# Attention heads emitted in steps, and the row of 1/rms spread behind the first transposes

## The chip, the cores and the metric

The kernel runs on one core of a Trainium2 chip. The metric is device time in microseconds (us) of one execution; lower is better. The engines have short names: PE (TensorE, matmuls and transposes), DVE (VectorE), ACT (ScalarE), POOL (GpSimd) and SP (SyncE, which issues the DMAs). Each engine works through its own list of instructions in order, and waits at an instruction until what it needs has been signalled by the others.

## The reference, cut to what matters

The program computes two layers of a decoder trunk in float32 on x of 512 tokens by 1024 features. Each layer is half an FFN, a mixer, half an FFN. The change lies in the mixer:

```python
h = rms_norm(x, mix_norm[l])
(nq, nkc, nvc, nks, nvs, nkw, nvw, ngate, sq, sk, sv, wq, wk, wv, bgate) = jnp.split(
    h @ w_in[l], SPLIT_POINTS, axis=-1)
y_nsa = nsa_attention(...)                       # 8 heads: compressed, selected, window
y_sb = stick_breaking_attention(sq, sk, sv)      # 4 heads, no softmax
y_swa = swa_sink_attention(wq, wk, wv, ...)      # 4 heads, window 128, sinks
g = sigmoid(bgate).reshape(B, S, 3, D)
merged = g[:, :, 0] * (y_nsa @ w_up_nsa[l]) + g[:, :, 1] * (y_sb @ w_up_sb[l]) + g[:, :, 2] * (y_swa @ w_up_swa[l])
x = x + merged @ w_out[l]
```

A stick-breaking head weighs key s for query t by beta_ts times the product of (1 - beta_tj) over s < j < t, with beta the sigmoid of the score; the product is a scan along a row. rms_norm divides each token by its root mean square; the kernel multiplies by 1/rms after the matmuls.

## The kernel before, in words

Matmuls are split into two parts: a float32 value a is hi + lo, with hi rounded to the matmul's short type by ACT (whi, ghi) and lo = a - hi by DVE (wlo, glo), and a product takes three matmuls (hi hi, lo hi, hi lo; lines 204 to 206 and 623 to 625). PE results go to eight PSUM banks of 128 partitions by 512 floats. `psum(...)` says which banks serve which kind of tile in turn: acc for accumulators, f for transposes and small products, s for scores, t for transposed weights, o for head outputs, c for the compress product. A tile waits until the last reader of the earlier tile in its bank is done.

`mix_front` emits the first part of the mixer of a layer: six projections `project(l, 0)` to `project(l, 5)` of h, each with four accumulators (one for each block of 128 tokens) over four loads of weights; after each, its accumulators are emptied (`evacuate`, DVE line 644, times 1/rms by a column, rcol), heads are normed and transposed, and heads of attention are emitted. `more(n)` adds early gates between them: `gate_early` makes one accumulator of gate logits (lines 204 to 206, from ghi and glo), multiplies it on DVE by the row of 1/rms (line 1045, tile gs), takes the sigmoid on ACT (line 1029) and stores it by SP into DRAM (gkept, line 1030). gs has one buffer. The first `more` makes two gates, in the first two acc banks, 4 and 5.

`nrm.means()` sums the squares by four small matmuls (line 242), works out rcol on DVE, and makes a diagonal of it (line 249, four instructions). `nrm.spread()` multiplies ones by that diagonal on PE (line 254), which gives 1/rms as a row in all partitions; ACT copies it out (line 256, tile rrow).

`transposed` (lines 682 to 693) makes hi and lo of the rows (ACT line 682, POOL line 683, tile st), transposes them on PE (line 691, tile f) and copies the result by ACT (line 693). sq has 16 such transposes, sk 32.

`stick_breaking` gives one head at a time: four scores (PE lines 716 and 717, tile s), two sigmoids of each (ACT lines 785 and 786), the diagonal block masked (POOL line 788, DVE line 789), the scan (DVE line 791), the product (POOL line 792, tile e); then the weights are transposed (PE lines 739 to 748, tile t), split (ACT line 727, DVE line 728, tile pt) and multiplied by v (PE line 733, tile o).

The whole is traced under `tile.TileContext(nc, schedule_with_timeline_sim=True)`: a scheduler decides the order on each engine from the emitted program, with the order of emission as a guide and its own costs. So the order of the code is not the order of the engines, and instructions are often drawn far ahead of where they are written.

Of the kernel before, what the change touches and what calls it, by code (L numbers as in the profile page):

```python
# [9 lines left out]
F32 = mybir.dt.float32  # L10
# [8 lines left out]
P = 128  # L19
# [75 lines left out]
def trunk(ctx, tc, I, out):  # L95
# [679 lines left out]
    def stick_breaking(q, k, v):  # L775

        for h in range(SBH):
# [3 lines left out]
            for t in range(NT):  # L781
# [11 lines left out]
                probs.append(beta)  # L793
            o = bank("o")
# [4 lines left out]
    def sliding(q, k, v, sinks):  # L799

        for h in range(SWH):
            if h % 2 == 0:
                y = unit("y")
            g = h // 2
            tab = unit("tt")[:, 0:SWW]
            rows = I["bias_rows"]
            sp.dma_start(tab, bass.AP(rows.tensor, rows.offset + (NH + h) * (RW + SRW) + RW, [[1, P], [1, SWW]]))
            neg = sm.tile([P, NT], F32, name=nm("neg"), tag="neg", bufs=3)
            den = sm.tile([P, NT], F32, name=nm("den"), tag="den", bufs=3)
            sk = sm.tile([P, NT], F32, name=nm("sk"), tag="sk", bufs=3)  # L810
            es = []
            for t in range(NT):
                p = bank("s")
                k0 = max(t - 1, 0) * P
                n = P if t == 0 else 256
                for i in range(2):
                    pe.matmul(p[:, 0:256], q[h][:, t * P : (t + 1) * P], k[g][i][:, k0 : k0 + 256], start=i == 0, stop=i == 1)
                e = unit(f"e{t}")[:, 0:n]
                dve.tensor_tensor_reduce(out=e, in0=p[:, 0:n], in1=tab[:, 0:n][:, ::-1], scale=-1.0, scalar=3e38, op0=ALU.add, op1=ALU.min, accum_out=neg[:, t : t + 1])
                es.append(e)  # L820

            dve.tensor_scalar(neg, neg, sinks[:, SWH + h : SWH + h + 1], None, ALU.min)
            dve.tensor_scalar(sk, neg, sinks[:, h : h + 1], None, ALU.add)
            for t in range(NT):
                exp(es[t], es[t], bias=neg[:, t : t + 1], scale=-1.0, accum_out=den[:, t : t + 1])
            exp(sk, sk)
            dve.tensor_tensor(den, den, sk, op=ALU.add)
            dve.reciprocal(den, den)
            for t in range(NT):
                pool.tensor_scalar(es[t], es[t], den[:, t : t + 1], 1.0, ALU.mult, ALU.mult)  # L830
            o = bank("o")
            pb = bank("t")
            pe.transpose(pb[:, 0:P], es[0], ident)
            pe.transpose(pb[:, P : 2 * P], es[1][:, 0:P], ident)
            pe.transpose(pb[:, 2 * P : 3 * P], es[1][:, P : 2 * P], ident)
            pe.transpose(pb[:, 3 * P : 4 * P], es[2][:, 0:P], ident)
            a = split_pt(pb, 0, 512)
            pb = bank("t")
            pe.transpose(pb[:, 0:P], es[3][:, P : 2 * P], ident)
            pe.transpose(pb[:, P : 2 * P], es[2][:, P : 2 * P], ident)  # L840
            pe.transpose(pb[:, 2 * P : 3 * P], es[3][:, 0:P], ident)
            b = split_pt(pb, P, 384)
            pv(o, v(g), 0, a, 0, 0, 256, True, False)

            for i, part in enumerate(b):
                pe.matmul(o[:, 256:512], v(g)[2], part[:, 256:512], start=False, stop=True, skip_group_check=True)
            for i, part in enumerate(a):
                pe.matmul(o[:, 128:384], v(g)[1], part[:, 256:512], start=False, stop=True, skip_group_check=True)
            for i, part in enumerate(b):
                pe.matmul(o[:, 256:512], v(g)[3], part[:, 0:256], start=False, stop=True, skip_group_check=True)  # L850
            finish_head(o, y, h)
            yield y
# [97 lines left out]
    def nsa(q, kk, v, vc, gates):  # L950
# [32 lines left out]
        ys = []  # L983
        for h in range(NH):
            if h % 2 == 0:
                y = unit("yn")
# [4 lines left out]
            o = bank("o")  # L991
# [18 lines left out]
            pool.tensor_tensor(e3, e3, den.unsqueeze(2).to_broadcast([P, NT, 32]), op=ALU.mult)  # L1010
            pb = bank("t")
# [6 lines left out]
            pe.matmul(o, vc[:, g].rearrange("p c d -> p (c d)"), part[0:64], start=True, stop=True, skip_group_check=True)  # L1018

            full_pv(o, scaled(chosen, h, 0), v(g), False, False)  # L1020
            full_pv(o, scaled(attend(h, kk[2 + g], tab), h, 1), v(2 + g), False, True)
            finish_head(o, y, h)
            if h % 2:
                ys.append(y)
# [42 lines left out]
    def mix_front(l, nrm, more):  # L1067
# [62 lines left out]
        for h, y in enumerate(sliding(wq, wk, wv, sinks)):  # L1130
            if h % 2:
                y_sw.append(y)
# [155 lines left out]
```

## Time and profile before

| | us |
|---|---|
| median of 3 runs | 2386.36 (2385.3 to 2389.08) |
| profiled execution, its own time | 2389.16 |
| its span | 2387.3 |
| PE busy | 2330.3 (98%) |
| DVE busy | 1749.4 (73%) |
| ACT busy | 1186.4 (50%) |
| POOL busy | 440.5 (18%) |
| mean granted clock of PE | 0.992 of full speed |

PE is busy in nearly the whole span, in every part of it; the other engines are full only in short stretches. In layer 0 the mixer's front begins near 393 us and its stick-breaking heads end near 545; in layer 1 the same comes some 1180 us later. The profiled execution is 2.8 us longer than the median.

### The profile page before, as it was taken

Reading aid. Unit: us, or ns where it says so; the run is one execution under the profiler, and the core shown is the slowest. Engines: PE = TensorE matmul, PEld = TensorE weight load, DVE = VectorE, ACT = ScalarE, POOL = GpSimd, SP = SyncE. Lnnn points to the kernel's source line nnn. Section 1 sums busy time; section 2 is a strip of 40 time slices with the busy share of each in tenths; the row PEclk is TensorE's granted clock in tenths of the full one; section 3 lists DMA queues with packets and bytes.
Section 4 is the critical chain, followed back from the end, with each engine's and each line's share of the span. In section 5 each row is a group of like instructions: output and inputs, shape, how many; then the busy total and the mean of one; then the engine's idle time right before and its main releaser. Section 6 shows DMA issues by size and latency. Waiting matters only on the chain.

```text
span 2387.3 us, 37809 instructions
## 1 busy us (share of the span) xinstructions
PE 2330.3 (98%) x14484; PEld 2066.2 (87%) x14484; DVE 1749.4 (73%) x3022; ACT 1186.4 (50%) x2145; POOL 440.5 (18%) x574
## 2 busy tenths in 40 slices
PE   8999999999999999999999999998999999999999
PEld 8988986887887799889899899778878878998997
DVE  8865864686777799658798568538867777994783
ACT  5533543454766555335455335335657664552451
POOL 1001001342333410010000100115234344001000
PEclk9999999999999999999999999999999999999999
DMA  4232333232323323323323332422423243233223
GB/s 160 96 106 82 103 118 112 76 124 91 98 94 119 115 80 107 104 83 107 109 86 105 111 96 87 144 79 86 143 70 104 77 140 102 74 112 109 96 90 96
DMA packets 83089, 244.15 MB, mean 102 GB/s; under 512 B 10197, under 2 KB 12034, under 8 KB 82908
## 3 DMA queue, kind: packets, MB, share of 16 engines
q1 hardware_dynamic: 82908, 241.73, 31.5%
q8 instruction: 114, 1.87, 0.3%
q14 instruction: 67, 0.55, 0.1%
HBM read 230.61 MB, written 11.08 MB: 101 GB/s over the span
## 4 chain that ended last, share of the span: by engine, by line
PE 88%; DVE 7%; issue 2%; ACT 1%; DMA 1%; POOL 1%; SPq 0%; DVEq 0%; ACTq 0%; POOLq 0%
PE X L392 20%; PE acc L206 13%; PE acc L204 13%; PE acc L205 12%; PE W L392 10%; PE Y L392 5%; PE acc L623 2%; PE acc L624 2%; PE acc L625 2%; PE o L733 2%; PE s L716 1%; PE s L717 1%; PE f L691 1%; DVE wlo L190 1%; PE c L891 1%
## 5 line engine op out<-in xcount | busy, mean ns | idle before, releaser
L189 ACT CAST whi<-wraw 128x1024 fp32r<-128x1024 f32 (+4 forms) x224 | 193.1, 866 | 397.3 <-PE acc L205 249.5
L190 DVE TENSOR_TENSOR wlo<-wraw,whi 128x1024 fp32r<-128x1024 f32 (+4 forms) x224 | 244.5, 1097 | 169.0 <-ACT whi L189 168.7
L392 ACT CAST whi<-u 128x1024 fp32r<-128x1024 f32 x156 | 163.8, 1050 | 283.0 <-DVE u L392 280.3
L204 PE MATMUL acc<-u,whi 128*128 128x512 f32 x704 | 276.9, 396 | 2.2 <-DVE gl L1150 2.2
L205 PE MATMUL acc<-u,whi 128*128 128x512 f32 x704 | 276.8, 394 | 0.0
L206 PE MATMUL acc<-u,wlo 128*128 128x512 f32 x704 | 276.6, 395 | 0.0
L392 DVE TENSOR_TENSOR wlo<-u,whi 128x1024 fp32r<-128x1024 f32 x164 | 204.5, 1247 | 14.8 <-ACT whi L392 14.3
L392 PE MATMUL X<-u,whi 128*128 128x256 f32 x1376 | 180.5, 284 | 3.7 <-ACT Y L392 3.0
L606 POOL TENSOR_TENSOR gl<-gl,e 128x512 f32<-128x512 f32 x32 | 55.9, 1747 | 690.7 <-DVE e L604 690.7
L392 PEld LDWEIGHTS X<-u,whi 128*128 128x128 f32 x1376 | 171.0, 189 | 7.0 <-ACT Y L392 3.4
L204 PE MATMUL acc<-u,ghi 128*128 128x512 f32 x384 | 162.3, 423 | 4.2 <-DVE gl L707 4.2
L206 PE MATMUL acc<-u,glo 128*128 128x512 f32 x384 | 159.5, 416 | 5.8 <-DVE glo L196 5.8
L204 PEld LDWEIGHTS acc<-u,whi 128*128 128x128 f32 x704 | 132.5, 188 | 34.3 <-DVE gl L1150 4.2
L206 PEld LDWEIGHTS acc<-u,wlo 128*128 128x128 f32 x704 | 132.4, 188 | 30.8
L205 PEld LDWEIGHTS acc<-u,whi 128*128 128x128 f32 x704 | 132.7, 188 | 30.2
L236 POOL TENSOR_TENSOR ssum<-ssum,e 128x512 f32<-128x512 f32 x42 | 58.8, 1399 | 541.0 <-issue 352.9
L205 PE MATMUL acc<-u,ghi 128*128 128x512 f32 x384 | 155.4, 405 | 0.0
L624 PE MATMUL acc<-wlo,u 128*128 128x512 f32 (+2 forms) x384 | 139.0, 363 | 0.3
L625 PE MATMUL acc<-whi,u 128*128 128x512 f32 (+2 forms) x384 | 137.3, 361 | 0.0
L623 PE MATMUL acc<-whi,u 128*128 128x512 f32 (+2 forms) x384 | 135.6, 364 | 0.0
L196 DVE TENSOR_TENSOR glo<-wraw,ghi 128x256 fp32r<-128x256 f32 x192 | 94.5, 494 | 53.5 <-ACT ghi L195 51.4
L604 DVE SCALAR_TENSOR_TENSOR e<-acc,rrow 128x512 f32<-128x512 f32 x64 | 44.2, 690 | 108.2 <-PE acc L206 108.2
(322 smaller groups left out, 5775.3 us busy)
## 6 DMA issues: line engine op xcount, KB each, us to landing
wraw<-in_wgu SPq DMA_DIRECT2D x104, 512.0 KB, 3.6
tt<-in_wgu SPq DMA_DIRECT2D x68, 512.0 KB, 3.6
wraw<-in_wd SPq DMA_DIRECT2D x64, 384.0 KB, 3.0
wraw<-in_wbg SPq DMA_DIRECT2D x48, 512.0 KB, 3.7
wraw<-in_wd SPq DMA_DIRECT2D x64, 320.0 KB, 2.9
wraw<-in_wup SPq DMA_DIRECT2D x16, 512.0 KB, 4.0
wraw<-in_wout SPq DMA_DIRECT2D x16, 512.0 KB, 3.6
tt<-rows_d SPq DMA_DIRECT2D x16, 456.0 KB, 4.6
```

The costliest lines, as they stand in the source:

```text
L189: marks["split"] = act.copy(hi, raw)
L190: dve.tensor_tensor(lo, raw, f32(hi), op=ALU.subtract)
L196: dve.tensor_tensor(lo, raw, f32(hi), op=ALU.subtract)
L204: pe.matmul(o, w[0], a[0], start=start, stop=False)
L205: pe.matmul(o, w[0], a[1], start=False, stop=False)
L206: pe.matmul(o, w[1], a[0], start=False, stop=stop)
L236: pool.tensor_tensor(self.sum, self.sum, sq, op=ALU.add)
L392: return lambda *a, **kw: tc.keep_in_program_order(getattr(self.engine, op)(*a, **kw))
L606: pool.tensor_tensor(x[d], x[d], e, op=ALU.add)
L623: pe.matmul(o, xh, w[0][:, j], start=k == 0, stop=False)
L624: pe.matmul(o, xh, w[1][:, j], start=False, stop=False)
L625: pe.matmul(o, xl, w[0][:, j], start=False, stop=k == KD - 1)
```

## The change

The stick-breaking generator yields between the scores of a head and its output, and `mix_front` takes the two halves at different places: scores of a head ahead of a projection, its output behind it. The fourth head's output stands behind `project(l, 4)`, so that this projection runs with fewer banks for f, and with t and o banks beside them. `nrm.spread()` is called after `transposed` of sq and sk instead of before `evacuate`. The sliding-window heads and the NSA heads become generators too, whose steps are called so that a head's scores are emitted ahead of the output of the head before.

```diff
@@ stick_breaking
                 probs.append(beta)
+            yield
             o = bank("o")
             full_pv(o, probs, v(h), True, True)
             finish_head(o, y, h)
             yield y
@@ mix_front
         nrm.means()
-        nrm.spread()
         rc = nrm.col
         raw = evacuate(b, 0, 512, rc)
         sq = transposed([r[:, 0:256] for r in raw], SBH, False, "u")
         sk = transposed([r[:, 256:512] for r in raw], SBH, True, "u")
+        nrm.spread()
         more(MORE[0])
         psum(acc=(4, 5, 0, 1), f=(7,), s=(2,), t=(3,), o=(6,))
         b = project(l, 1, nrm)
         sv = v_prepare(b, 0, SBH, rc, "u")
         raw = evacuate(b, 256, 256, rc, "gl")
+        sb = stick_breaking(sq, sk, sv)
+        next(sb)
         blks = [blocks(l, [r[:, i * P : (i + 1) * P] for r in raw], which) for i, which in enumerate("kv")]
-        sb = stick_breaking(sq, sk, sv)
-        y_sb = [None, next(sb)]
         more(MORE[1])
         b = project(l, 2, nrm)
+        y_sb = [next(sb)]
...
-        y_sb[0] = next(sb)
+        next(sb)
         head_norms(raw, SWH, rows[:, 5])
-        next(sb)
         more(MORE[2])
         b = project(l, 3, nrm)
+        next(sb)
         raw_k = evacuate(b, 0, 128, rc)
         wv = v_prepare(b, 128, 2, rc, "gl")
+        next(sb)
         wq = transposed(raw, SWH, False, "gl")
         raw = raw_k
-        y_sb[1] = next(sb)
+        more(MORE[3])
+        y_sb.append(next(sb))
         head_norms(raw, 2)
+        next(sb)
         wk = transposed(raw, 2, True, "yn")
-        more(MORE[3])
-        psum(acc=(4, 5, 0, 1), f=(3, 7, 6), c=(2,))
+        psum(acc=(4, 5, 0, 1), f=(7,), t=(3,), o=(6,), c=(2,))
         p = bank("c")
         b = project(l, 4, nrm, lambda g: [compress_in(l, c, blks, p) for c in COMPRESS[g]])
+        next(sb)
+        psum(acc=(4, 5, 0, 1), f=(3, 7, 6))
...
@@ the sliding-window heads, at the end of mix_front (the NSA heads alike)
-        for h, y in enumerate(sliding(wq, wk, wv, sinks)):
-            if h % 2:
-                y_sw.append(y)
+        hs = [sliding(h, wq, wk, wv, sinks, y_sw) for h in range(SWH)]
+        next(hs[0])
+        for h in range(SWH):
+            if h + 1 < SWH:
+                next(hs[h + 1])
+            next(hs[h])
```

Both programs have the same instructions on every engine; only their order and banks differ, and that only from the first early gate to the end of the fifth projection in each layer. The three places below are on PE in layer 0.

First, the last group of sk's transposes (L691, f tiles from st tiles) with the accumulators of the second projection (acc_4165 to acc_4168 in both kernels). Before:

```order
L625 MATMUL acc_4166<-whi_4171,u_3386 128x512
L623 MATMUL acc_4166<-whi_4171,u_3438 128x512
L624 MATMUL acc_4166<-wlo_4172,u_3438 128x512
L625 MATMUL acc_4166<-whi_4171,u_3438 128x512
L623 MATMUL acc_4166<-whi_4201,u_3491 128x512
L624 MATMUL acc_4166<-wlo_4202,u_3491 128x512
L625 MATMUL acc_4166<-whi_4201,u_3491 128x512
L691 MATMUL f_4045<-ident_r,st_4033 128x128
L623 MATMUL acc_4166<-whi_4201,u_3544 128x512
L691 MATMUL f_4045<-ident_r,st_4036 128x128
```

In the changed kernel, the end of the same transposes:

```order
L691 MATMUL f_4061<-ident_r,st_4032 128x128
L691 MATMUL f_4061<-ident_r,st_4035 128x128
L691 MATMUL f_4048<-ident_r,st_4038 128x128
L691 MATMUL f_4061<-ident_r,st_4038 128x128
L254 MATMUL f_4067<-e_578_3940,tri 128x512
L716 MATMUL s_4306<-u_4008,u_3970 128x256
L717 MATMUL s_4306<-u_4008,u_3970 128x256
L623 MATMUL acc_4165<-whi_4171,u_3386 128x512
L624 MATMUL acc_4165<-wlo_4172,u_3386 128x512
L625 MATMUL acc_4165<-whi_4171,u_3386 128x512
```

Before, matmuls of acc_4166 stand ahead of these transposes and among them, and the spread (L254) was 130 rows ahead. Now the transposes stand in one run, the spread follows them, then the first score of the first stick-breaking head (L716, L717), and acc_4165 only begins behind it.

Second, the last score of the first stick-breaking head (before: s_4401, then s_4633 is the next head's; e_684 its last weights) and what follows. Before, at the end of the projection of wqg (acc_4497 to acc_4500):

```order
L624 MATMUL acc_4500<-wlo_4594,u_3756 128x280
L625 MATMUL acc_4500<-whi_4593,u_3756 128x280
L716 MATMUL s_4633<-u_4025,u_3974 128x256
L717 MATMUL s_4633<-u_4025,u_3974 128x256
L739 MATMUL t_4413<-tri,e_684_4404 128x128
L204 MATMUL acc_4834<-u_3386,ghi_4837 128x512
L205 MATMUL acc_4834<-u_3386,ghi_4837 128x512
```

In the changed kernel, that head's last score (s_4339) at the end of the second projection:

```order
L624 MATMUL acc_4168<-wlo_4262,u_3756 128x512
L625 MATMUL acc_4168<-whi_4261,u_3756 128x512
L716 MATMUL s_4339<-u_4008,u_3970 128x512
L717 MATMUL s_4339<-u_4008,u_3970 128x512
L739 MATMUL t_4584<-tri,e_665_4331 128x128
L858 MATMUL f_4350<-tri,gl_4299 128x128
```

The last weights of that head (e_684 before) were transposed some 50 rows behind their score; now the score is right behind the second projection, and its weights (e_668) are transposed over 100 rows later.

Third, the last two stick-breaking heads ahead of the compress product (c tile). Before (o_4796 is the third head's output):

```order
L733 MATMUL o_4796<-pt_4813,u_4289 128x384
L746 MATMUL t_4818<-tri,e_767_4788 128x128
L748 MATMUL t_4818<-tri,e_764_4777 128x128
L748 MATMUL t_4818<-tri,e_767_4788 128x128
L891 MATMUL c_5261<-whi_5328,gl_4318 128x256
L891 MATMUL c_5261<-wlo_5329,gl_4318 128x256
```

In the changed kernel (o_5069 is the third head's output, t_5461 holds the fourth head's weights):

```order
L691 MATMUL f_5216<-ident_r,st_5189 128x128
L691 MATMUL f_5216<-ident_r,st_5192 128x128
L733 MATMUL o_5069<-pt_5095,u_4290 128x256
L733 MATMUL o_5069<-pt_5096,u_4290 128x256
L733 MATMUL o_5069<-pt_5095,u_4290 128x256
L733 MATMUL o_5069<-pt_5096,u_4290 128x256
L739 MATMUL t_5461<-tri,e_841_5142 128x128
L739 MATMUL t_5461<-tri,e_844_5153 128x128
L890 MATMUL c_5223<-whi_5290,gl_4363 128x256
L890 MATMUL c_5223<-wlo_5291,gl_4363 128x256
```

Before, the third head's last transposes come right before the compress product, and its last output matmuls 22 matmuls behind its start; now all its output matmuls, and the transposes of wk (f_5216), stand ahead of it.

## Rows read from the trace of the kernel before

**Rows 1.** The page: span; chain that ended last, shares by engine

```profile
span 2387.3 us, 37809 instructions
...
PE 88%; DVE 7%; issue 2%; ACT 1%; DMA 1%; POOL 1%; SPq 0%; DVEq 0%; ACTq 0%; POOLq 0%
```

**Rows 2.** Waits of PE: line <- releaser: us in total, times, longest

```profile
PE f L254 <- DVE e L249: 10.1, 2, 5.7
...
PE t L739 <- POOL e L792: 6.1, 4, 2.2
```

**Rows 3.** Timeline, first layer, 397 to 403: start, duration, engine, line, tile [idle before]

```profile
397.66 0.87 DVE L249 TENSOR_SCALAR e<-tri,rcol 128x128 f32<-128x128 f32 x4
...
398.44 2.72 DVE L644 TENSOR_SCALAR rw<-acc,rcol 128x512 f32<-128x512 f32 x4
...
398.59 1.97 PE L254 MATMUL f<-e,tri 128*128 128x512 f32 x2 [4.36 <-DVE e L249]
...
399.57 1.41 PE L204 MATMUL acc<-u,ghi 128*128 128x512 f32 x1
...
400.78 0.63 PE L205 MATMUL acc<-u,ghi 128*128 128x512 f32 x1
...
400.85 0.58 ACT L256 COPY rrow<-f 128x512 f32<-128x512 f32 x1
...
401.21 0.63 PE L206 MATMUL acc<-u,glo 128*128 128x512 f32 x1
...
402.80 0.39 PE L205 MATMUL acc<-u,ghi 128*128 128x512 f32 x1
...
403.03 0.39 PE L206 MATMUL acc<-u,glo 128*128 128x512 f32 x1
```

**Rows 4.** Timeline, last two groups of transposes of sk, 420 to 429

```profile
420.64 0.69 DVE L1045 TENSOR_TENSOR gs<-acc,rrow 128x512 f32<-128x512 f32 x1 [0.77 <-PE acc L206]
...
422.30 0.45 PE L691 MATMUL f<-ident_r,st 128*128 128x128 f32 x4
...
425.24 0.74 POOL L683 TENSOR_TENSOR st<-rw,st 128x256 fp32r<-128x256 f32 x1
...
427.67 0.97 PE L691 MATMUL f<-ident_r,st 128*128 128x128 f32 x10
...
428.33 1.07 ACT L693 CAST u<-f 128x512 fp32r<-128x512 f32 x2 [0.46 <-PE f L691]
```

**Rows 5.** DMA issues: tile, queue, count, KB each, us to landing

```profile
gkept<-gs SPq DMA_DIRECT2D x18, 256.0 KB, 2.0
```

**Rows 6.** Timeline, 462 to 489: PE behind its waits; DVE ahead of the last

```profile
462.50 0.33 PE L739 MATMUL t<-tri,e 128*128 128x128 f32 x1 [2.24 <-POOL e L792]
...
485.16 0.57 DVE L789 TENSOR_TENSOR e<-e,tri 128x128 f32<-128x128 f32 x1
...
485.76 1.20 DVE L791 TENSOR_TENSOR_SCAN e<-e 128x128 f32<-128x128 f32 x1
...
486.74 0.33 PE L739 MATMUL t<-tri,e 128*128 128x128 f32 x1 [0.81 <-POOL e L792]
...
489.14 0.77 PE L204 MATMUL acc<-u,ghi 128*128 128x512 f32 x1 [2.08 <-DVE gl L707]
```

**Rows 7.** Windows: length, busy of PE, PEld, DVE, ACT, POOL, PE clock, DMA, GB/s

```profile
410.00:440.00 30.00, 30.00 (x154) 24.55 (x153) 8.43 (x17) 15.45 (x32) 6.01 (x11) 1.00 0.18 57
...
461.54:488.99 27.45, 23.47 (x153) 21.30 (x153) 25.59 (x52) 15.28 (x40) 17.62 (x22) 0.91 0.30 96
...
490.00:500.00 10.00, 10.00 (x40) 8.04 (x40) 7.92 (x23) 4.82 (x14) 3.14 (x5) 0.79 0.43 150
```

**Rows 8.** Timeline, last stick-breaking heads, 511 to 520

```profile
511.64 0.40 DVE L789 TENSOR_TENSOR e<-e,tri 128x128 f32<-128x128 f32 x1 [1.04 <-ACT e L786]
...
517.62 0.39 PE L891 MATMUL c<-whi,gl 128*128 128x256 f32 x1
...
519.87 0.53 DVE L728 TENSOR_TENSOR pt<-t,pt 128x384 fp32r<-128x384 f32 x1
```

More of the change, by code (lines that the diff above doesn't have):

```diff
@@ L797, in stick_breaking @@
             yield y
[L799 to L852, printed above, removed]
@@ new lines, in sliding @@
+    def sliding(h, q, k, v, sinks, ys):
+        g = h // 2
+        tab = unit("tt")[:, 0:SWW]
+        rows = I["bias_rows"]
+        sp.dma_start(tab, bass.AP(rows.tensor, rows.offset + (NH + h) * (RW + SRW) + RW, [[1, P], [1, SWW]]))
+        neg = sm.tile([P, NT], F32, name=nm("neg"), tag="neg", bufs=3)
+        den = sm.tile([P, NT], F32, name=nm("den"), tag="den", bufs=3)
+        sk = sm.tile([P, NT], F32, name=nm("sk"), tag="sk", bufs=3)
+        es = []
+        for t in range(NT):
+            p = bank("s")
+            k0 = max(t - 1, 0) * P
+            n = P if t == 0 else 256
+            for i in range(2):
+                pe.matmul(p[:, 0:256], q[h][:, t * P : (t + 1) * P], k[g][i][:, k0 : k0 + 256], start=i == 0, stop=i == 1)
+            e = unit(f"e{t}")[:, 0:n]
+            dve.tensor_tensor_reduce(out=e, in0=p[:, 0:n], in1=tab[:, 0:n][:, ::-1], scale=-1.0, scalar=3e38, op0=ALU.add, op1=ALU.min, accum_out=neg[:, t : t + 1])
+            es.append(e)
+        dve.tensor_scalar(neg, neg, sinks[:, SWH + h : SWH + h + 1], None, ALU.min)
+        dve.tensor_scalar(sk, neg, sinks[:, h : h + 1], None, ALU.add)
+        for t in range(NT):
+            exp(es[t], es[t], bias=neg[:, t : t + 1], scale=-1.0, accum_out=den[:, t : t + 1])
+        exp(sk, sk)
+        dve.tensor_tensor(den, den, sk, op=ALU.add)
+        dve.reciprocal(den, den)
+        for t in range(NT):
+            pool.tensor_scalar(es[t], es[t], den[:, t : t + 1], 1.0, ALU.mult, ALU.mult)
+        yield
+        o = bank("o")
+        pb = bank("t")
+        pe.transpose(pb[:, 0:P], es[0], ident)
+        pe.transpose(pb[:, P : 2 * P], es[1][:, 0:P], ident)
+        pe.transpose(pb[:, 2 * P : 3 * P], es[1][:, P : 2 * P], ident)
+        pe.transpose(pb[:, 3 * P : 4 * P], es[2][:, 0:P], ident)
+        a = split_pt(pb, 0, 512)
+        pb = bank("t")
+        pe.transpose(pb[:, 0:P], es[3][:, P : 2 * P], ident)
+        pe.transpose(pb[:, P : 2 * P], es[2][:, P : 2 * P], ident)
+        pe.transpose(pb[:, 2 * P : 3 * P], es[3][:, 0:P], ident)
+        b = split_pt(pb, P, 384)
+        pv(o, v(g), 0, a, 0, 0, 256, True, False)
+        for i, part in enumerate(b):
+            pe.matmul(o[:, 256:512], v(g)[2], part[:, 256:512], start=False, stop=True, skip_group_check=True)
+        for i, part in enumerate(a):
+            pe.matmul(o[:, 128:384], v(g)[1], part[:, 256:512], start=False, stop=True, skip_group_check=True)
+        for i, part in enumerate(b):
+            pe.matmul(o[:, 256:512], v(g)[3], part[:, 0:256], start=False, stop=True, skip_group_check=True)
+        finish_head(o, ys[h // 2], h)
+        yield
@@ L981, in scaled, with head @@
             return es
[L983 to L986, printed above, removed]
+        def head(h, y, o):
             g = h // 4
@@ L1017, in nsa @@
             dve.tensor_tensor(part[32:64], pb[0:32], f32(part[0:32]), op=ALU.subtract)
[L1018 to L1022, printed above, removed]
-            if h % 2:
-                ys.append(y)
+            pe.matmul(o[0], vc[:, g].rearrange("p c d -> p (c d)"), part[0:64], start=True, stop=True, skip_group_check=True)
+            full_pv(o[0], chosen, v(g), False, False)
+            yield
+            full_pv(o[0], window, v(2 + g), False, True)
+            finish_head(o[0], y, h)
+            yield
+        ys = [unit("yn") for _ in range(NH // 2)]
+        hs = [head(h, ys[h // 2], []) for h in range(NH)]
+        next(hs[0])
+        for h in range(NH):
+            next(hs[h])
+            next(hs[h])
+            if h + 1 < NH:
+                next(hs[h + 1])
+            next(hs[h])
         return ys
```

12 lines of the change are left out of this document (9 added, 3 removed).

## The prediction

> **What bounds the kernel now.** I read the page's span and chain first, then the list of what TensorE waited for, then the stretches around those waits in order of time. The page shows a kernel that TensorE sets: 2387.3 us of span, 88% of the closing chain on PE [rows 1]. So the change can win only the time in which PE stands, plus what a low clock costs behind a stand. The list of waits says where PE stands. Of the lines that the change touches, two entries lead: 10.1 us in two waits of the spread's matmul (L254) for DVE's diagonal (L249), and 6.1 us in four waits of the transposes L739 for POOL [rows 2]. They come in pairs, one for each layer, so I work out layer 0 and double it.
>
> One part of the change drops out at once. The instructions of the sliding and NSA heads stand in the same order, engine by engine, in both kernels: the scheduler had already put the next head's scores ahead of the previous head's outputs. Rewriting them as steps changes nothing, and their waits stay. What really moves lies between the first projection and the fifth: the spread, and the four stick-breaking heads.
>
> **Term A, the spread leaves the front.** Before, L254 waits 4.36 us for the diagonal, starts at 398.59, and the clock is low: two L204-type matmuls start 0.43 us apart (400.78, 401.21) where 0.23 is normal (402.80, 403.03) [rows 3]. 0.43 to 0.23 is the ratio of the 1.2 GHz level to the 2.4 GHz level. The first early-gate matmul behind it is through at 400.78, so it had really begun at about 400.78 - 0.43 = 400.35. In the new order that gate matmul comes first. It needs no diagonal, but its bank is the one that the first evacuation (L644) empties, and this stands on DVE right behind the diagonal, in both kernels: 398.44 + 2.72/4 = 399.12 [rows 3], with the handoff 399.2. The wait is thus renamed, not removed; PE gains 400.35 - 399.2 = 1.1 us. Bounds: 0.3 (its start taken as the trace gives it, 399.57 [rows 3]) to 1.3. **A = -1.1.**
>
> **Term B, the spread's new place.** L254 now stands behind all 48 transposes of sq and sk. The two early gates need its row, and until DVE has multiplied by it they hold two of the four accumulator banks. So two of the four accumulators of the second projection (acc_4165 and acc_4166, 18 matmuls each ahead of the last weights) cannot start. Before, acc_4166's matmuls lay among the last group of transposes and covered them; now nothing covers them. The chain is read from that stretch of before [rows 4], with T = 422.30, the start of the second-last group's transposes: POOL's last subtraction ends at 425.24 + 0.74 = T + 3.7; the transpose behind it and half of the 1.07 us of two ACT casts: T + 4.35; L254 about 1.0 us (half of its 1.97 us at the low clock): T + 5.35; ACT's copy of the row, 0.58 [rows 3]; DVE's product, 0.69; four handoffs, 0.3 together: the projection may go on at about T + 7.0. In the same time PE has 4 transposes (0.45), 16 more at 0.97 for ten (1.55), two matmuls (0.5) and L254 itself (1.0), less overlap about 3.2 us. That leaves a wait of 3.8 us (2.8 to 5.0, by shorter handoffs or L254 at the low clock). To it comes L254's own 1.0 us, which the front no longer pays, and some six matmuls at the low clock, 6 x 0.20 = 1.2 us (0 to 1.6). **B = +6.0**, between 3.8 and 8.6. The second gate's product waits until the first gate's store has left the single buffer: 2.0 us to landing [rows 5]. It ends some 4.9 us behind the row, and the 18 matmuls of acc_4165 and the scores beside them last to 5.3, so I cost it at nothing. On SP that store now stands behind one more weight load, which has been issued long before; I cost that at nothing too. If the cover goes, it is rival 3.
>
> The Trainium skill speaks against this step (Perfetto Trace Analysis, section Matmuls): independent groups of matmuls should rotate through PSUM banks, so that the evacuation of one runs beside the matmuls of the next. The trace of before agrees, since at 420.64 DVE empties a gate's bank [rows 4] while PE goes on. By that rule alone the sign of B is plus; its size comes from the rows above.
>
> **Term C, stick-breaking heads 0 and 1.** Before, PE waits 2.24 us at 462.50 for head 0's last weights, and 0.81 and 2.08 us at 486.74 and 489.14 [rows 6], 5.1 us together. The new order has head 0's last score right behind project 1 (it stood in the middle of project 2), so the first wait goes. But between 461.54 (first evacuation of project 2) and 488.99 (the end of the L707 that releases PE) DVE is busy 25.6 of 27.45 us [rows 7]. DVE has the same work there in the new kernel, but for two instructions of the next head that move behind it, 0.57 + 1.20 us [rows 6]. So the stretch up to 489.14, 27.6 us, shrinks to some 23.8 us of DVE plus 1.4 us of gaps and handoffs (1.85 were idle before), 25.2: what PE does not wait at 462 it waits at the end, for wlo and for L707. **C = -2.4**; bounds 0 and -5.1 (all three waits gone). The slow clock behind that wait (0.79 in 490 to 500 [rows 7]) I leave as it is.
>
> **Term D, the last stick-breaking heads.** Before, DVE ran without a break from 511.64 to 519.87 + 0.53 = 520.40, twelve instructions, the last of them the L728 for the third head's output; PE did not notice, because the compress product (L891) had begun at 517.62 and its matmuls stood ahead of that output [rows 8]. In the new order the output stands ahead of the compress product. Had nothing else moved, PE would wait 520.40 - 517.62 = 2.8 us. DVE's chain is shorter there (the long scan of the last head and an output's sum lie elsewhere), but nine of the projection's matmuls fewer stand behind the transposes, 9 x 0.23 = 2.1 us of PE work less. I take about half of the 2.8: **D = +1.5**; bounds 0 (DVE's shorter chain decides) and 4.0 (all of the 2.8 and six matmuls at the low clock).
>
> **The sum.** A + B + C + D = -1.1 + 6.0 - 2.4 + 1.5 = +4.0 us per layer, +8 for both. The profiled run took 2389.16 us with 1.9 us outside its span, 2.8 above the median of 2386.36; the change in span is carried over, so 2397 for such a run and 2394 for the median. With every term at its better end it is -1.3 + 3.8 - 5.1 + 0 = -2.6 a layer, with every one at its worse end -0.3 + 8.6 + 0 + 4.0 = +12.3; ends seldom meet, so the forecast's own range is 2386 to 2404.
>
> **Rivals.** 1. *The heads' split does what interleaving is for: faster.* For it: the waits at 462, 486 and 489 are direct, and the last leaves the clock at 0.79 for ten us [rows 7], which costs 0.21 x 10 = 2.1. If DVE is ahead when project 3 is evacuated, because its instructions get shorter where POOL is quiet, C is -5.1 - 2.1, D is 0 and B its lower end, +3.8, with A -1.1: -4.5 a layer, 2386.4 - 9 = 2377 us. Against it: DVE's 25.6 busy us. The Trainium skill speaks for it (Perfetto Trace Analysis, section Optimization Strategy): where the most contended engine changes over time, interleaving the regimes may help; the trace agrees that there are such regimes, DVE 25.6 of 27.45 us busy in one and 8.4 of 30 in 410 to 440 [rows 7]. 2. *The waits only change names: no difference.* B at 2.8 of wait and no clock loss, C -2.9, D 0: -1.1 + 3.8 - 2.9 = -0.2 a layer, 2386. For it: A, where just that happens. 3. *The store decides: much slower.* If the first gate's store lands over half a us later than 2.0, acc_4166 waits too; 2 us more to landing is 1.5 us a layer and as much of slow clock, 2394 + 6 = 2400 or more. For it: one buffer, and SP's queue; against it: a median of 2.0 over 18 stores [rows 5].
>
> **How the numbers follow.** Two runs of this kernel can be told apart from about 0.2%, 4.8 us. Forecast 0.55, of which 0.08 lies within 0.2%; rival 1 0.20; rival 2 0.17; rival 3 0.08. Slower: 0.47 + 0.08 = 0.55; same: 0.17 + 0.08 = 0.25; faster: 0.20. The range goes from 2377, which leaves out the half of rival 1 beyond its own time, to 2405, which leaves out the far part of rival 3.
>
> **What would show it.** A: the first early-gate matmul waits 4.5 to 5.2 us, released by L644. B: waits of 3 to 5 us in all between the last transposes and the second projection, the last of them on DVE's gate product, in both layers. C: no wait of L739 near 462, one of 1 to 3 us at the end of project 3. D: a wait of the output matmuls L733 on pt ahead of the compress product. I am wrong if B's wait is absent or under 1.5 us, or if project 3 ends without a wait; then rival 1 holds.

## The result, and the profile after

The changed kernel takes 2401.93 us (median of 5 runs, 2397.35 to 2403.76); the kernel before took 2388.35 us beside it (5 runs, 2385.3 to 2390.21). The ratio is 1.0061, 95% interval 1.0049 to 1.0072: slower by 0.6%, some 13.6 us. The forecast was slower, 2394 us with a range to 2405: the side was right. The time is 8 us short, of which 2 us are the median of before (2386.36 when the forecast was made); the difference, +8 against +13.6, is 5.6 short. The profiled run has 12.8 us more of span than [rows 1], and PE's share of the chain is the same.

The page of the changed kernel, span and closing chain:

```profile
span 2400.1 us, 37819 instructions
...
PE 88%; DVE 7%; ACT 2%; issue 2%; DMA 1%; POOL 0%; SPq 0%; DVEq 0%; ACTq 0%; POOLq 0%
```

PE's waits in the changed kernel (line <- releaser: us in total, times, longest), to be read beside [rows 2]:

```profile
PE acc L204 <- DVE rw L644: 11.3, 2, 6.2
PE acc L206 <- DVE glo L196: 6.7, 2, 3.3
...
PE acc L204 <- DVE gl L707: 5.0, 2, 2.5
...
PE o L733 <- DVE pt L728: 3.3, 3, 1.2
...
PE acc L624 <- DVE wlo L190: 1.9, 2, 1.1
...
PE s L716 <- ACT rrow L256: 1.4, 2, 0.7
...
PE f L254 <- ACT u L693: 1.2, 2, 0.6
```

The waits of L254 for the diagonal and of L739 for POOL have left the head of the list. In their place stand the gate's wait at the front (L644), the waits around the late spread (rrow, u), and those for wlo, L707 and pt. The list does not say what they cost, because a low clock follows some of them. So I made a ledger of the first layer from the windows view: standing time is a window's length less PE's busy time; the cost of the low clock is length times (1 - granted clock), in pieces of 10 us. A clock that is low while PE stands is counted in both (at the front it is 0.5 of the 3.4 us in the changed kernel, 1.9 of the 3.5 with heads 0 and 1 whole). The columns are fixed in time, so the work of a kernel that is some us ahead shifts to the left in them. Each cell is stand / low clock in us.

| kernel | 390-420 | 420-440 | 440-520 | 520-580 | 580-620 | sum |
|---|---|---|---|---|---|---|
| before | 4.4 / 1.7 | 0 / 0 | 5.9 / 5.1 | 0 / 0 | 2.9 / 1.7 | 13.1 / 8.5 |
| changed | 5.0 / 3.4 | 1.8 / 3.4 | 5.2 / 1.7 | 0.9 / 0 | 3.4 / 3.4 | 16.3 / 11.9 |
| late spread alone | 5.0 / 3.4 | 1.8 / 3.4 | 2.9 / 0 | 0 / 0 | 3.3 / 1.7 | 13.1 / 8.5 |
| steps alone | 4.4 / 3.4 | 0 / 0 | 5.3 / 0 | 0 / 0 | 3.3 / 1.7 | 13.0 / 5.1 |
| heads 0, 1 whole | 5.0 / 3.5 | 1.7 / 3.4 | 2.6 / 0 | 0 / 0 | 3.3 / 1.7 | 12.6 / 8.6 |
| gate in bank 6 | 0.1 / 0 | 0 / 0 | 4.5 / 0 | 0 / 0 | 3.3 / 1.7 | 7.9 / 1.7 |

Before to changed it is +6.6 us. Where the NSA heads begin (L206 for glo: 593.65 before, 600.33 now) the changed kernel is 6.7 us late; up to there the ledger has +4.9, since 1.7 us of its clock lie behind that wait. Most of the rest is standing that the view does not see: it counts gaps inside a group of instructions as busy (the stand of 3.8 us below shows as 1.8), so a cell may be up to 2 us short. Up to the NSA heads, then, more of the loss is standing than clock.

The second layer begins 7.2 us late (its front wait begins at 1574.67 before, 1581.89 now). In the same pieces, from 1570 to 1800, it goes from 15.0 / 8.5 to 16.4 / 10.3, and its L206 is 14.0 us late (1774.78 before, 1788.81 now). Behind that wait the clock falls only before, and the whole span ends 12.8 us longer.

The front of the changed kernel, first layer (start, duration, engine, line, tile, idle before), beside [rows 3]:

```profile
399.02 0.80 PE L204 MATMUL acc<-u,ghi 128*128 128x512 f32 x1 [5.03 <-DVE rw L644]
...
403.88 0.63 PE L206 MATMUL acc<-u,glo 128*128 128x512 f32 x1
...
405.06 0.39 PE L624 MATMUL acc<-wlo,u 128*128 128x512 f32 x1
```

The gate waits for its bank, and the 12 of its matmuls that run first are 0.43 us apart, the 1.2 GHz level; the 2.4 GHz level is back only near 405. Before, it was back by 402.80 [rows 3].

The late spread, 423 to 431, beside [rows 4]:

```profile
423.36 0.45 PE L691 MATMUL f<-ident_r,st 128*128 128x128 f32 x4
...
424.18 1.81 PE L691 MATMUL f<-ident_r,st 128*128 128x128 f32 x10
...
426.27 0.73 POOL L683 TENSOR_TENSOR st<-rw,st 128x256 fp32r<-128x256 f32 x1
...
428.01 1.36 PE L254 MATMUL f<-e,tri 128*128 128x512 f32 x2 [0.59 <-ACT u L693]
429.42 0.59 ACT L256 COPY rrow<-f 128x512 f32<-128x512 f32 x1 [0.97 <-PE f L254]
...
430.03 0.69 DVE L1056 TENSOR_TENSOR gs<-acc,rrow 128x512 f32<-128x512 f32 x1 [7.71 <-ACT rrow L256]
430.05 0.58 PE L716 MATMUL s<-u,u 128*128 128x256 f32 x1 [0.68 <-ACT rrow L256]
...
430.78 0.79 PE L623 MATMUL acc<-whi,u 128*128 128x512 f32 x1
```

This is the chain of term B, link by link. From 424.18 to 430.78, 6.6 us, PE has 1.55 us of transposes, 1.0 of L254 and 0.24 of scores to do: it stands 3.8 us, as forecast. This counts the work at full clock, as the forecast does; L254 took 1.36 us and the scores 0.73, so some 0.8 us of the 3.8 are slow work. Its projection begins 0.06 us after the gate product (430.03 + 0.69) has freed the bank. Note the L716 at 430.05, head 0's first scores: before, they came at 439.04, behind the projection's matmuls.

The end of project 3, 485 to 494, beside [rows 6]:

```profile
485.67 1.15 DVE L190 TENSOR_TENSOR wlo<-wraw,whi 128x512 fp32r<-128x512 f32 x1
...
486.84 0.33 SPq L171 DMA_DIRECT2D wraw<-in_wi_nkv  x1
...
488.88 0.35 DVE L644 TENSOR_SCALAR rw<-acc,rcol 128x128 f32<-128x128 f32 x1
...
490.64 1.04 ACT L189 CAST whi<-wraw 128x1024 fp32r<-128x1024 f32 x1 [5.03 <-PE f L691]
491.59 0.36 ACT L706 ACTIVATE gl<-acc,rcol 128x128 fp32r<-128x128 f32 x1
491.72 1.22 DVE L190 TENSOR_TENSOR wlo<-wraw,whi 128x1024 fp32r<-128x1024 f32 x1 [2.49 <-ACT whi L189]
...
492.86 0.34 DVE L644 TENSOR_SCALAR rw<-acc,rcol 128x128 f32<-128x128 f32 x1
493.12 0.34 DVE L707 SCALAR_TENSOR_TENSOR gl<-acc,rcol,gl 128x128 fp32r<-128x128 f32 x1
...
493.61 0.76 PE L204 MATMUL acc<-u,ghi 128*128 128x512 f32 x1 [2.45 <-DVE gl L707]
```

Read it from below. The gate waits for L707, which frees its bank. L707 stands behind a weight split (L190, 491.72) on DVE and, by way of L706, behind that split's cast (L189, 490.64) on ACT. The cast is put down to PE, but the load of its weights was issued at 486.84, when the split of 485.67 had freed the buffer, and such loads of 512 KB take about 4 us here: the cast starts 3.8 us after the issue. So the evacuation of finished work queues, on both engines, behind weights of the next project that are still on their way.

In the kernel before, the split stands ahead of L707 too, but its load was issued in time, and DVE did not stand in front of it:

```profile
479.20 1.16 DVE L190 TENSOR_TENSOR wlo<-wraw,whi 128x512 fp32r<-128x512 f32 x1
...
480.38 0.33 SPq L171 DMA_DIRECT2D wraw<-in_wi_nkv  x1
...
487.26 1.22 DVE L190 TENSOR_TENSOR wlo<-wraw,whi 128x1024 fp32r<-128x1024 f32 x1
```

Counted from the first evacuation of project 2 (461.54 before, 467.92 now), the split that frees the buffer stands where it stood, 17.7 us behind. It is PE that comes to its wait for L707 earlier, 23.2 us behind where it was 25.5, since it no longer waits 2.24 us at 462, and so it meets the load.

The windows that answer to [rows 7] (length, busy of PE, PEld, DVE, ACT, POOL, PE clock, DMA, GB/s):

```profile
420.00:440.00 20.00, 18.23 (x74) 13.26 (x73) 4.22 (x8) 9.70 (x20) 4.63 (x11) 0.83 0.07 27
...
467.92:493.46 25.54, 21.81 (x150) 19.74 (x149) 22.70 (x50) 13.15 (x33) 14.03 (x18) 1.00 0.33 103
```

The second is the stretch of term C: DVE is busy for 22.70 us and idle for 2.84, of which 2.49 is the one stand at 491.72.

The last heads, beside [rows 8]:

```profile
519.57 0.50 PE L733 MATMUL o<-pt,u 128*128 128x512 f32 x1 [1.24 <-DVE pt L728]
...
524.43 0.62 PE L733 MATMUL o<-pt,u 128*128 128x256 f32 x3 [0.86 <-DVE pt L728]
525.02 0.36 PE L890 MATMUL c<-whi,gl 128*128 128x256 f32 x1
```

The outputs stand ahead of the compress product, and wait 2.1 us.

### The profile page after: what moved, and what is told of

It reads as the page before. It is cut to its first block, busy times and chain, and to the rows that moved or that the text cites. A ratio compares the mean times of both kernels' runs of the same rounds, so it can differ in the third digit from the quotient of the medians.

```text
span 2400.1 us, 37819 instructions
## 1 busy us (share of the span) xinstructions
PE 2338.8 (97%) x14484; PEld 2069.2 (86%) x14484; DVE 1742.0 (73%) x3022; ACT 1187.1 (49%) x2145; POOL 431.4 (18%) x574
## 4 chain that ended last, share of the span: by engine, by line
PE 88%; DVE 7%; ACT 2%; issue 2%; DMA 1%; POOL 0%; SPq 0%; DVEq 0%; ACTq 0%; POOLq 0%
PE X L392 20%; PE acc L204 12%; PE acc L206 12%; PE acc L205 12%; PE W L392 10%; PE Y L392 5%; PE acc L623 3%; PE acc L624 2%; PE acc L625 2%; PE o L733 2%; PE s L716 1%; PE s L717 1%; DVE wlo L190 1%; PE f L691 1%; PE t L739 1%
## 5 line engine op out<-in xcount | busy, mean ns | idle before, releaser
L189 ACT CAST whi<-wraw 128x1024 fp32r<-128x1024 f32 (+4 forms) x224 | 192.8, 867 | 400.1 <-PE acc L205 249.9
L190 DVE TENSOR_TENSOR wlo<-wraw,whi 128x1024 fp32r<-128x1024 f32 (+4 forms) x224 | 243.4, 1094 | 161.7 <-ACT whi L189 161.7
L206 PE MATMUL acc<-u,wlo 128*128 128x512 f32 x704 | 276.4, 395 | 0.0
L206 PE MATMUL acc<-u,glo 128*128 128x512 f32 x384 | 158.0, 412 | 6.7 <-DVE glo L196 6.7
L206 PEld LDWEIGHTS acc<-u,wlo 128*128 128x128 f32 x704 | 132.3, 188 | 31.0
```

The lines of the kernel that those rows point to most:

```text
L189: marks["split"] = act.copy(hi, raw)
L190: dve.tensor_tensor(lo, raw, f32(hi), op=ALU.subtract)
L206: pe.matmul(o, w[1], a[0], start=False, stop=stop)
```

## Experiments

Differences are between medians, against the kernel before in the same series of runs.

**One half at a time.** The spread alone, in the kernel before:

```diff
         nrm.means()
-        nrm.spread()
...
         sk = transposed([r[:, 256:512] for r in raw], SBH, True, "u")
+        nrm.spread()
         more(MORE[0])
```

> The kernel before with one edit: the spread of the row of 1/rms stands behind all transposes of sq and sk, as in the changed kernel; the heads stay as before. My theory (terms A and B, as the trace of after has them: A about +0.4 to +1.1 us a layer, B about +6.5): +6 to +8 a layer, so 12 to 16 us above the kernel before, ratio 1.005 to 1.007; the projection begins behind a stand of about 3.8 us that ends on DVE's gate product, and the clock falls behind it. Rival 1 (the stand is a matter of the heads, whose first scores now stand ahead of the projection): within 2 us of before. Rival 2 (it is the heads' split that costs, the spread costs half): +3 to +7.

Measured: 2389.85 against 2387.68 us, ratio 1.0008 (1.0000 to 1.0016), +2 us where I expected +12 to +16. And the steps alone (the changed kernel with the opposite edit):

> The changed kernel with the spread put back at the front: only the heads in steps are left. My theory (terms C and D, C about -2.4 to -3.1 us a layer, D about +1.5 to +1.7): -1 a layer, so -2 us against before, 2384 to 2388 when before is at 2388, ratio 0.998 to 1.000; no wait of L739 near 462, but one of 2 to 4 us at the end of project 3, and about 2 us of waits of L733 for pt ahead of the compress product. Rival (the heads' steps cost by themselves): ratio 1.002 or more. Rival (interleaving works once the spread is out of the way): 0.997 or less, 7 us faster.

Measured: 2383.29 us, ratio 0.9988 (0.9979 to 0.9998), -4 us. Each half is harmless or better; together they cost 13.6. So a sum of parts was the wrong model. In the spread-only kernel term B is there in full (see the ledger, 420-440), but the waits of [rows 6] are nearly gone. Its first scores, in the timeline:

```profile
430.36 0.58 PE L716 MATMUL s<-u,u 128*128 128x256 f32 x1 [0.68 <-ACT rrow L256]
```

And from its list of PE's waits, both layers:

```profile
PE t L739 <- POOL e L792: 0.9, 2, 0.5
...
PE acc L204 <- DVE gl L707: 0.7, 2, 0.4
```

While the projection has no bank, PE does head 0's first scores, 8.7 us earlier than before. DVE, ACT and POOL then work on the head beside the projection, and in 440 to 520 standing and clock fall from 5.9 / 5.1 to 2.9 / 0 us. In the ledger that pays for B.

**Which heads.** The changed kernel with heads 0 and 1 whole (heads 2 and 3 still in steps, the spread late):

```diff
+        blks = [blocks(l, [r[:, i * P : (i + 1) * P] for r in raw], which) for i, which in enumerate("kv")]
         sb = stick_breaking(sq, sk, sv)
         next(sb)
-        blks = [blocks(l, [r[:, i * P : (i + 1) * P] for r in raw], which) for i, which in enumerate("kv")]
+        y_sb = [next(sb)]
         more(MORE[1])
         b = project(l, 2, nrm)
-        y_sb = [next(sb)]
...
         next(sb)
+        next(sb)
         head_norms(raw, SWH, rows[:, 5])
         more(MORE[2])
         b = project(l, 3, nrm)
-        next(sb)
```

> The changed kernel with the first two stick-breaking heads emitted whole again, each at its old place; the late spread and the steps of heads 2 and 3 stay. The runs so far: the spread alone +2 us, the steps alone -4, both +14, so the parts do not add. Theory 1 (the late spread alone already lets head 0's scores in ahead of the second projection, 9 us earlier, so the wait near 462 is gone without any steps, and the steps of heads 0 and 1 then only push DVE's work back): this kernel is faster than the changed one by 4 us or more, 2392 to 2398 when that one is at 2402. Theory 2 (terms add as predicted; with C undone, 1.9 to 2.4 us a layer are lost): 2405 to 2408.

Measured: 2388.08 against 2388.06 us, ratio 1.0002 (0.9993 to 1.0011). The 13.6 us are gone, within some 2 us: they lie in the steps of heads 0 and 1, given the late spread. Its end of project 3 shows the split of the next weights behind the evacuation, and PE waiting 0.37 us:

```profile
488.19 0.33 DVE L707 SCALAR_TENSOR_TENSOR gl<-acc,rcol,gl 128x128 fp32r<-128x128 f32 x1
...
488.67 0.47 PE L204 MATMUL acc<-u,ghi 128*128 128x512 f32 x1 [0.37 <-DVE gl L707]
...
489.64 1.22 DVE L190 TENSOR_TENSOR wlo<-wraw,whi 128x1024 fp32r<-128x1024 f32 x1
```

The last head whole and ahead of the fifth projection (the changed kernel with the second `next(sb)` of that head moved up):

> The changed kernel with the last stick-breaking head emitted whole and ahead of the fifth projection, as before, so that its output no longer stands beside the compress product; the rest of the change stays. Term D (the waits of the output matmuls for pt ahead of the compress product, 1.24 and 0.86 us) says: -1.5 to -3.3 us a layer, 2395 to 2399 when the changed kernel is at 2402. Rival (those waits only change places): within 1.5 us of the changed kernel.

Measured: 2402.47 us, ratio 1.0066 (1.0053 to 1.0078), no gain. Its waits for pt are the same, so they are not the last head's:

```profile
520.12 0.50 PE L733 MATMUL o<-pt,u 128*128 128x512 f32 x1 [1.23 <-DVE pt L728]
...
524.98 0.62 PE L733 MATMUL o<-pt,u 128*128 128x256 f32 x3 [0.87 <-DVE pt L728]
```

With heads 0 and 1 whole, where the same work comes some 5 us earlier, one wait of 0.59 us for pt is left in the first layer, at 514.75. So most of that waiting goes with the steps of the first heads and is no term of its own.

**What holds PE at the end of project 3.** First, less work for DVE in the same order (the kernel leaves out three quarters of one product):

```diff
-            dve.tensor_tensor(v, v, r[:, t].unsqueeze(2).to_broadcast([P, nh, DH]), op=ALU.mult)
+            dve.tensor_tensor(v[:, 0 : m or nh], v[:, 0 : m or nh], r[:, t][:, 0 : m or nh].unsqueeze(2).to_broadcast([P, m or nh, DH]), op=ALU.mult)
...
-        head_norms(raw, SWH, rows[:, 5])
+        head_norms(raw, SWH, rows[:, 5], 1)
```

> The changed kernel in the same order, with four VectorE instructions of each layer cut to a quarter of their width: the product of the sliding heads' queries with the heads' 1/rms is done for one head of four (that part of the computation is left out). They stand in the stretch that ends with the waits of 1.07 and 2.45 us in front of project 3's end (L624 for wlo, L204 for L707); four times 0.70 us becomes about four times 0.25. Theory (the stretch is bound by DVE, as term C says): the waits shrink by 1.8 us a layer and the clock stays up behind them, -2 to -4 us a layer, 2394 to 2398 when the changed kernel is at 2402. Rival (the wait is for a chain of several engines, DVE's busy time is not the bound): -0.5 us a layer or less, 2401 to 2402.

Measured: 2396.82 us, ratio 1.0043 (1.0030 to 1.0056): +8.8 us, 4.8 less than the changed kernel. The four L662 took 1.45 us where they took 2.79, the wait for wlo went, and that for L707 fell to 1.77. So DVE's work counts, as the theory says, but at least in part by way of the load: with the shorter work the load is issued at 484.31, where it was 486.84, and DVE still stands 2.50 us in front of the split. Then the order on DVE's queue alone (`marks["lo"]` is the split L190, `marks[0]` the first L707):

```diff
-            w = load(f"wi_{name}", (l, g), 2, n)
+            w = load(f"wi_{name}", (l, g), 2, n); gi == 4 and g == 1 and behind(marks["lo"], marks[0])
```

> The changed kernel with one order fixed on VectorE's queue: the split of the fifth projection's second weight block (wlo, L190) stands behind the first L707 of project 3's evacuation, not ahead of it. In the trace of the changed kernel DVE stands 2.49 us idle in front of that split (its weights were only just loaded), the evacuations queue behind it, and PE's next gate waits 2.45 us for their bank. Theory (a head-of-line block of one instruction makes the last wait of term C): that wait falls to 0.5 us or less and the clock stays up behind it, -2 to -4 us a layer, 2394 to 2398 when the changed kernel is at 2402. Rival (DVE is bound there by its busy time, so the same time is waited somewhere in the next 20 us): within 1.5 us of the changed kernel.

Measured: 2398.22 us, ratio 1.0043 (1.0029 to 1.0057): +10.1 us, 3.5 less than the changed kernel. Its trace shows why only a part went:

```profile
491.34 1.05 ACT L189 CAST whi<-wraw 128x1024 fp32r<-128x1024 f32 x1 [5.00 <-PE f L691]
492.29 0.36 ACT L706 ACTIVATE gl<-acc,rcol 128x128 fp32r<-128x128 f32 x1
...
492.69 0.35 DVE L707 SCALAR_TENSOR_TENSOR gl<-acc,rcol,gl 128x128 fp32r<-128x128 f32 x1 [2.47 <-ACT gl L706]
...
493.18 0.47 PE L204 MATMUL acc<-u,ghi 128*128 128x512 f32 x1 [1.29 <-DVE gl L707]
```

The same block stands on ACT's queue. With the cast behind the first L706 too:

> The changed kernel with the block taken off both queues: on DVE the split of the fifth projection's second weight block, and on ACT its cast (L189), stand behind the first piece of project 3's evacuation. In the run with DVE's order alone the gate's wait fell from 2.45 to 1.29 us, and DVE's L707 then waited 2.47 us for ACT's L706, which stood behind the cast of weights that were still being loaded. Theory (the block is on ACT's queue too): the wait at the end of project 3 falls below 0.5 us, 1 to 4 us under the run before, 2394 to 2397. Rival (what is left is DVE's busy time): 2398 to 2399, the wait still over 1 us.

Measured: 2394.69 against 2387.39 us, ratio 1.0031 (1.0020 to 1.0042): +7.3 us, 6.3 less than the changed kernel. The gate no longer waits, and the cast is now put down to the load:

```profile
488.38 0.37 ACT L706 ACTIVATE gl<-acc,rcol 128x128 fp32r<-128x128 f32 x1 [3.65 <-DVE rw L644]
...
488.78 0.35 DVE L707 SCALAR_TENSOR_TENSOR gl<-acc,rcol,gl 128x128 fp32r<-128x128 f32 x1 [0.18 <-ACT gl L706]
...
489.74 1.05 ACT L189 CAST whi<-wraw 128x1024 fp32r<-128x1024 f32 x1 [0.80 <-DMA wraw<-in_wi_nkv]
490.12 0.47 PE L204 MATMUL acc<-u,ghi 128*128 128x512 f32 x1
```

So by the medians nearly half of the 13.6 us is this block: 6.3 us, uncertain by some 4 (the two profiled runs are 4.3 us apart). The edit did not move these two instructions alone: the scheduler also placed later work anew. On POOL three of the splits L683 now stand ahead of the longest product L792, which in the changed kernel came first (511.76, and L683 from 515.64):

```profile
509.78 3.13 POOL L683 TENSOR_TENSOR st<-rw,st 128x256 fp32r<-128x256 f32 x3 [0.32 <-ACT st L682]
512.86 2.12 POOL L792 TENSOR_TENSOR e<-e,e 128x511 f32<-128x511 f32 x1
```

PE waits 1.36 us for that product at 515, and 1.07 for ACT at 513, in the place of the two waits for pt. So the block may be worth more than this run shows. These waits and one of 0.84 us for wlo at 486 are what is left; whether they make up all of the rest stays open.

**The banks.** No early gate ahead of the second projection:

```diff
-MORE = (2, 1, 1, 1, 1, 3)
+MORE = (0, 3, 1, 1, 1, 3)
```

> The changed kernel with no early gate ahead of the second projection (two of them moved behind the blocks, ahead of the third projection). It tests whether term B's stand comes from the two gates that hold accumulator banks until the row is there. My theory: all four accumulators of the second projection are free, its matmuls cover the transposes and the spread's chain, the stand of 3.8 us between the last transposes and the projection goes, and with it the 4.5 us at the low clock: -5 to -7 us a layer, 2388 to 2392 when the changed kernel is at 2402. The wait at the front stays (the projection's first accumulator waits for the same evacuation). Rival (the row's chain itself is what is waited for, by whatever comes next, or the gates are missed as cover of the transposes): 2400 to 2404.

Measured: 2389.95 against 2387.68 us, ratio 1.0013 (1.0004 to 1.0021), 11 us under the changed kernel. The projection then runs ahead of the spread, with no low clock in 420 to 440 (1.00, where the changed kernel has 0.83). At the end of project 3 PE no longer waits for L707 either (one wait of 1.93 us for ACT's L693 stands at 491.50). So these 11 us and the 6.3 above overlap, and are not shares of one sum. And the reverse, a bank more at the front of the kernel before:

```diff
-        psum(acc=(4, 5, 0, 1), f=(7, 2, 3))
+        psum(acc=(4, 5, 0, 1), f=(7, 2, 3), g=(6,))
...
-        g = gate_logits(l, i, nrm, "gs")
+        g = gate_logits(l, i, nrm, "gs", "g" if i == 0 else "acc")
...
-        p = bank("acc")
+        p = bank(bk)
```

> The kernel before, with the first early gate's accumulator in PSUM bank 6, which is free at that place, in place of one of the four banks that the first evacuation empties. The gate's 24 matmuls (24 x 0.23 = 5.6 us) can then run while PE waits for the diagonal of 1/rms (4.4 and 5.7 us in the two layers). My theory: the two waits shrink to under 1 us and the clock does not fall there, -4 to -6 us a layer unless the transposes then lack those matmuls as cover: 2376 to 2382 when before is at 2388. Rival (the work was only moved: the same stand comes back a few us later, in front of the casts of ACT and POOL that feed the transposes): 2386 to 2389.

Measured: 2368.28 against 2387.68 us, ratio 0.9918 (0.9904 to 0.9931), -19 us where I expected -6 to -12. The gate's 24 matmuls fill the whole wait:

```profile
390.00:420.00 30.00, 29.89 (x147) 23.19 (x145) 11.76 (x32) 12.76 (x27) 6.12 (x8) 1.00 0.29 90
```

The clock stays at 1.00 there, and in 440 to 520 too. The Trainium skill's rule that I cited against B (Perfetto Trace Analysis, section Matmuls: rotate independent groups through PSUM banks) is borne out here: one bank more for one group is worth more than the whole change costs. The same edit in the changed kernel:

> The changed kernel with the first early gate's accumulator in the free PSUM bank 6. Term A says that the front wait was renamed: the gate's first matmul waits for the bank that the first evacuation empties. Theory: with a bank of its own the gate's 24 matmuls fill the 5.0 and 6.2 us, and the clock does not fall there; it also gives the second projection one accumulator more while the row is late, so part of term B goes as well: -7 to -12 us a layer, 2378 to 2388 when the changed kernel is at 2402. Rival (the matmuls taken from behind are missed between the transposes, where the spread is late and PE already stands 3.8 us): -2 us a layer or less, 2398 to 2402.

Measured: 2396.62 us, ratio 1.0038 (1.0025 to 1.0050), 5 us under the changed kernel. The front wait is 0.86 us, but in 420 to 440 stand and low clock grow to 4.2 / 6.8: the matmuls that moved forward are missed where the spread is late.

**Both things that helped.** The gate in bank 6 and the heads in steps, the spread early:

> The kernel before with both things that helped alone: the first early gate in PSUM bank 6 (-19 us alone) and the stick-breaking heads in steps (-4 alone); the spread stays at the front. If they add: 2364. Theory (as with the late spread, whatever lets head 0's scores in earlier has already taken what the steps can give, and the steps then push work onto DVE where it is full): 2368 to 2375, no better than the gate alone.

Measured: 2374.87 against 2388.13 us, ratio 0.9944 (0.9931 to 0.9956): 6 us worse than the gate alone. With the split behind the evacuation:

> The kernel of the run before (gate in bank 6, heads in steps, spread at the front) with the split of the fifth projection's second weight block behind the first evacuation, as in the other run. If the steps' cost is that block on DVE's queue: 2 to 6 us below the run before. If not: the same within 1.5 us.

Measured: 2366.69 us, ratio 0.9912 (0.9899 to 0.9926), 8 us less, somewhat more than expected. It is level with the gate alone; both beat the kernel before by 0.8 to 0.9%.

## Why the prediction was right in sign and short in size

- **A (-1.1).** The wait was renamed as said: released by L644, 5.03 us where 4.5 to 5.2 stood, the gate from 399.02 where 399.2 stood. The gain of 1.1 us was there where the gate began (6.1 us behind the start of the wait before, 5.0 now), and was lost behind it. From the start of the front wait to the second-last transposes the first layer lost 1.3 us (394.23 to 422.30 before, 393.99 to 423.36 now); the second gained 0.5. I had taken the low clock behind the wait as unchanged. That is the mis-sized part: in windows of 0.5 us, without the time in which PE stood, it cost 2.9 us in the first layer where it had cost 1.7, and 2.3 in the second where it had cost 3.1. Whether the order has a part in this stays open: with the spread early and the heads in steps, the first layer's cost was 2.4.
- **B (+6.0).** Right by its steps: POOL ends at T + 3.64 (said 3.7), the projection begins at T + 7.42 (7.0), PE stands 3.8 us (3.8), the last to release it is the gate product. Up to project 2's first evacuation (461.54 before, 467.92 now) it is 6.4 less the 1.1 that T was late, +5.3 (+5.1 in the second layer). What failed is B as a cost of the spread: the spread-only run has the same stand and is 2 us slower, not 12.
- **C (-2.4).** The stretch went from 27.6 to 25.7 us, where 25.2 stood. But the gain is not the steps', once the spread is late: the late spread alone brings head 0's scores forward and wins more. The step that failed is "the new order has head 0's last score right behind project 1", credited to the heads. Given the late spread, the steps of heads 0 and 1 cost all of the 13.6 us. And the length came out right by another sum: 22.7 us of DVE and one stand of 2.49, not 23.8 and 1.4 of gaps. What bound the stretch was the chain from the freed buffer over load, cast and split to L707, and not DVE's busy time alone.
- **D (+1.5).** The waits came on the line named (1.24 and 0.86 us), and the delay grew by 1.7 us, from 4.5 at the gate of 493.61 to 6.2 at the gate behind the compress product (539.30 before, 545.51 now); in the second layer by 2.7. But with heads 0 and 1 whole only 0.59 us is left of them in the first layer, and with the last head whole they stay: most of them goes with the first heads' steps.
- **The sum (+4 a layer, measured nearly +7).** The terms follow the line of time. In the first layer the delay grew by +1.1, +5.3, -1.9 and +1.7, which is 6.2 at the gate behind the compress product: within 1 us of each term but for A, which is 2.2 off by its clock. In the second layer it grew by -0.5, +5.1, -1.0 and +2.7, which is 6.3: there C is 1.4 and D 1.2 us off. L206's wait for glo, which I did not reckon with, adds 0.5 us in each; the clock behind it cost 1.7 us more than before in the first layer (3.4 for 1.7) and 1.7 less in the second (0 for 1.7). As shares of the two parts of the change the terms were wrong: by A + B the spread alone costs 9.8 us in both layers and by C + D the steps gain 1.8, where the runs have +2 and -4, and no term stands for what the two do together. That the side and the rough size still came out is in part luck.
- **Rivals.** Rival 1 (the steps work) is what happens with the spread early, -4 us; the rule on interleaving that the Trainium skill gives (Perfetto Trace Analysis, section Optimization Strategy) thus held for one order of the rest and not for the other. Rival 2's "waits change names" fits the spread alone. Rival 3: no wait in PE's list was set by the gate's store; DVE waited 0.74 us for it, at 433.99, ahead of the second gate's product, and costing that at nothing was right.

## What to carry to other kernels

Two edits that take from the same slack do not add: run each alone and both, before the gain of the pair is put down to either. Before interleaving heads, look at each in-order queue for a weight split or cast that stands ahead of an evacuation: while its load is on the way, it keeps a PSUM bank, and with it the matmul engine. And when the matmul engine waits for a bank, a free bank for work that needs nothing from the late operand is the first thing to try; in the kernel before it was worth 19 us, more than any order alone, and in the changed kernel still 5.

## What was not expected of the hardware

The same stand costs a different amount of clock from run to run. PE's wait of 3.3 us for glo (L206) cost none in the second layer of the changed kernel (its window around that wait; the clock column is 1.00):

```profile
1780.00:1790.00 10.00, 6.66 (x32) 4.74 (x31) 8.98 (x18) 3.21 (x11) 6.48 (x5) 1.00 0.10 31
```

In the first layer of the kernel with the late spread alone, the clock was 0.83 over ten us, a cost of 1.7 us:

```profile
590.00:600.00 10.00, 6.66 (x28) 5.26 (x27) 7.91 (x15) 2.90 (x8) 8.59 (x8) 0.83 0.32 95
```

And in the kernel without early gates ahead of project 1 it was 0.66, a cost of 3.4 us:

```profile
590.00:600.00 10.00, 6.69 (x23) 5.53 (x23) 6.80 (x15) 2.63 (x7) 7.47 (x7) 0.66 0.33 94
```

Nor did the shorter stands order themselves by length: 1.93 us at 491.50 in that same kernel left the clock at 1.00, and three stands of 1.3 us together, in 500 to 510 of the last kernel of the experiments, came with a clock of 0.83. Part of a fall can also be over before PE works again: 0.6 of the 3.4 us above lay in the wait itself. So a forecast made stand by stand is uncertain by some 2 us at each, in either direction; mine gave the clock one value per stand.
